# A float16 batched matmul with subtraction on one core: clearing the idle matmuls' operands on GpSimd, and another place for VectorE's first visit

## The chip, the cores and the metric

One core of one Trainium2 chip. The time is the device time of one execution in microseconds. The kernel before takes 210.94 us (median of 6 runs, 210.65 to 211.54, beside the changed kernel). The times inside a profile count from the first instruction of one profiled execution; this span (208.7 us in the kernel before) is some 2 us shorter than the device time.

## The reference

```python
batch, m, k, n = 16, 512, 1024, 768      # all float32
def reference(x, weight, sub_value):
    return (np.matmul(x, weight) - sub_value).astype(np.float32)
```

The 16 x 512 rows are 64 tiles of 128 rows. Inputs and outputs make 87 MB.

## The kernel before

SyncE issues all transfers from one queue, in a fixed order: x into a ring of 16 tiles, sub_value into a ring of 32, weights in 4 chunks, and outputs from the sub_value ring. ScalarE casts x to float16. The transposition is done by PE for most tiles and by VectorE for a pair of tiles in six. PE multiplies, and VectorE subtracts from PSUM into the ring. Three accumulators take turns.

Two parts matter here. First, PE does idle matmuls on zeros at the start, to bring its clock up before the first tile; in the kernel before, VectorE clears the zeros as the first thing of its program:

```python
starts = len(dve.ops)
dve.add(lambda: nc.vector.memset(idle_w, 0.0), then=count("idle"))
dve.add(lambda: nc.vector.memset(idle_x, 0.0), then=count("idle"))
dve.ops = dve.ops[starts:] + dve.ops[:starts]

def idle(n):
    pe.add(lambda: nc.tensor.ldweights(idle_w, tile_position=(0, 0)), [(counter["idle"], 2)])
    for _ in range(n):
        pe.add(lambda: loaded_matmul(po_b[:, NPO - 1, 0], idle_w, idle_x, start=True, stop=True))
...
idle(13)
cast(0)
pe.add(...one more idle matmul..., [(counter["ident"], 2)])
transpose_tile(0)
```

Second, PE, ScalarE and VectorE do not go straight into their work. Each first branches to the block behind it ("past"), then comes back, so that this place of its program is fetched early (called its first visit below):

```python
with nc.body("turn_head", valid_engines=engines):
    nc.br_cmp(turn, 0, on_true="past", on_false="work", comp_op="IS_EQ", engines=engines)
with nc.body("work", valid_engines=engines):
    for q in (act, dve):
        q.emit(q.ops)
    ...                                   # PE's program
    nc.br("past", engines=engines)
with nc.body("past", valid_engines=engines):
    nc.regs_alu(turn, turn, 1, op=mybir.AluOpType.add)
    nc.br_cmp(turn, 2, on_true="turn_head", on_false="rest", comp_op="IS_LT", engines=engines)
nc.switch_bb("rest")
```

## Time and profile before

| | kernel before |
|---|---|
| profiled span | 208.7 us |
| PE busy | 196.2 us, 94% |
| DMA queue of all transfers | 97.9% of 16 engines' span, 417 GB/s |
| VectorE's wait after its first branch | 3.99 us |
| idle matmuls start | 6.07 us |
| last subtraction starts | 204.08 us |
| last output issued, landed | 205.06, 207.37 us |

The first page line of the prediction below is PE's busy tenths in 40 equal slices. DMA in the second is the mean over 16 engines.

### The profile page before, as it was taken

To read this page: it belongs to the slowest core of one execution; us is meant where nothing else is said; L and a number is where in the kernel's file an instruction comes from. 1 tells how busy PE (TensorE), PEld (TensorE's weight loads), DVE (VectorE), ACT (ScalarE), POOL (GpSimd) and SP (SyncE) were. 2 spreads that over 40 slices of the span, in tenths; PEclk is the share of its full clock that TensorE was granted. 3 is DMA by queue.
4 is the path that set the end of the run, shared out by engine and by line. 5 is a ranking of instruction groups with operands and counts; after the bars stand their busy time and mean duration, and the time that the engine had idled before them with its cause. 6 is when DMAs were issued, how large, how long until landed. Compare 5 with 4: busy or idle time off the path is not lost.

```text
span 208.7 us, 2630 instructions
## 1 busy us (share of the span) xinstructions
PE 196.2 (94%) x1234; PEld 75.6 (36%) x700; DVE 127.6 (61%) x218; ACT 108.9 (52%) x113; POOL 0.8 (0%) x7
## 2 busy tenths in 40 slices
PE   0899979999999999999999999999999999999991
PEld 0023324434433443443443344344344334434430
DVE  0231151995696599299469559929946955982331
ACT  2246478554762845557276284555727629434510
POOL 1000000000000000000000000000000000000000
PEclk9999999999999999999999999999999999999997
DMA  6999999999999999999999999999999999999985
GB/s 205 407 426 429 436 422 433 443 419 437 438 422 457 400 438 443 446 427 407 460 433 415 424 429 433 441 440 432 416 452 415 435 424 429 438 438 419 423 350 211
DMA packets 5476, 87.08 MB, mean 417 GB/s; under 512 B 608, under 2 KB 608, under 8 KB 1888
## 3 DMA queue, kind: packets, MB, share of 16 engines
q1 hardware_dynamic: 5472, 87.03, 97.9%
q14 instruction: 3, 0.02, 0.1%
q8 instruction: 1, 0.02, 0.0%
HBM read 61.87 MB, written 25.17 MB: 417 GB/s over the span
## 4 chain that ended last, share of the span: by engine, by line
PE 92%; ACT 3%; issue 2%; DVE 1%; DVEq 0%; SPq 0%
PE po_b L181 82%; PE pt_b L318 10%; ACT x_b L300 1%; ACT xt_b L331 1%; ACT xtp_b L331 0%; DVE so_ring L400 0%; DVE idle_x L411 0%; DVE idle_w L410 0%; DVEq L507 0%; DVEq L519 0%; DVEq L518 0%; DVEq L555 0%; DVEq L504 0%; SPq L133 0%
## 5 line engine op out<-in xcount | busy, mean ns | idle before, releaser
L181 PE MATMUL po_b<-w_sb,xt_b 128*128 128x384 f16 x704 | 125.9, 326 | 0.0
L400 DVE TENSOR_TENSOR so_ring<-po_b,so_ring 128x768 f32<-128x768 f32 x64 | 61.2, 958 | 60.0 <-PE po_b L181 53.8
L331 ACT COPY xt_b<-pt_b 128x1024 f16<-128x1024 f16 x44 | 44.5, 1012 | 80.3 <-PE pt_b L318 79.0
L351 DVE STREAM_TRANSPOSE xtp_b<-x16p_b 32x256 f32<-32x256 f32 x144 | 62.7, 435 | 2.2
L181 PE MATMUL po_b<-w_sb,xtp_b 128*128 128x384 f16 x320 | 61.3, 326 | 0.1
L380 PEld LDWEIGHTS <-xt_b 128*128 128x128 f16 x352 | 34.4, 98 | 57.2 <-issue 53.7
L318 PE MATMUL pt_b<-ident,x_b 128*128 128x128 f32 x184 | 47.6, 274 | 1.6 <-ACT x_b L300 1.4
L300 ACT CAST x_b<-x_ring 128x1024 f16<-128x1024 f32 x46 | 47.2, 1048 | 2.9 <-DMA x_ring<-in_x_dram 2.9
L318 PEld LDWEIGHTS pt_b<-ident,x_b 128*128 128x128 f32 x184 | 25.4, 141 | 46.1 <-issue 42.4
L380 PEld LDWEIGHTS <-xtp_b 128*128 128x128 f16 x160 | 15.7, 98 | 18.5 <-issue 16.4
L300 ACT CAST x16p_b<-x_ring 128x1024 f16<-128x1024 f32 x18 | 18.8, 1046 | 4.0 <-DMA x_ring<-in_x_dram 4.0
L181 PE MATMUL po_b<-idle_x,idle_w 128*128 128x512 f16 x26 | 9.2, 513 | 6.1 <-DVE idle_x L411 6.1
L248 DVE CAST w_sb<-so_ring 128x768 f16<-128x768 f32 x8 | 4.1, 556 | 9.6 <-DMA so_ring<-in_weight_dram 9.6
L410 DVE MEMSET idle_w<- 128x64 uint32 x1 | 0.1, 112 | 5.6 <-issue 5.6
L331 ACT COPY xtp_b<-pt_b 128x1024 f16<-128x1024 f16 x2 | 2.0, 1012 | 2.2 <-PE pt_b L318 2.2
L415 PEld LDWEIGHTS <-idle_w 128*128 128x128 f16 x4 | 0.4, 99 | 6.1 <-DVE idle_x L411 6.1
L300 ACT ACT_TABLE_LOAD x1 | 1.3, 1283 | 1.8 <-issue 1.8
L487 ACT CAST stub<-ident 128x1 f16<-128x1 f32 x2 | 0.4, 196 | 0.0
L170 POOL TENSOR_SCALAR_AFFINE_SELECT ident<-ident 128x128 f32<-128x128 f32 x1 | 0.3, 292 | 0.1
L411 DVE MEMSET idle_x<- 128x256 uint32 x1 | 0.3, 272 | 0.0
L464 POOL MEMSET mark<- 128x1 f32 x1 | 0.1, 99 | 28.6 <-ACT xtp_b L331 28.6
L169 POOL MEMSET ident<- 128x128 f32 x1 | 0.2, 204 | 0.5 <-SPq L133 0.5
(4 smaller groups left out, 0.4 us busy)
## 6 DMA issues: line engine op xcount, KB each, us to landing
so_ring<-in_sub_value_dram SPq DMA_DIRECT2D x7, 3072.0 KB, 24.3
out_dram<-so_ring SPq DMA_DIRECT2D x7, 3072.0 KB, 24.5
x_ring<-in_x_dram SPq DMA_DIRECT2D x5, 4096.0 KB, 20.7
x_ring<-in_x_dram SPq DMA_DIRECT2D x2, 2048.0 KB, 27.1
so_ring<-in_weight_dram SPq DMA_DIRECT2D x4, 768.0 KB, 9.6
x_ring<-in_x_dram SPq DMA_DIRECT2D x1, 3072.0 KB, 24.8
x_ring<-in_x_dram SPq DMA_DIRECT2D x2, 1024.0 KB, 23.2
out_dram<-so_ring SPq DMA_DIRECT2D x1, 1920.0 KB, 7.7
```

What stands on the lines that cost most here:

```text
L170: pool.add(lambda: nc.gpsimd.affine_select(out=ident, in_=ident, compare_op=mybir.AluOpType.not_equal, fill=1.0, base=0, pattern=[[-1, P]] ...
L181: return nc.tensor.add_instruction(mybir.InstMatmult(name=nc.get_next_instruction_name(), engine=full.engine, ins=list(full.ins), outs=lis ...
L248: lambda at=at, r=r, st=st: nc.vector.tensor_copy(out=w_sb[:, at, r], in_=st[:, r]),
L300: act.add(lambda: nc.scalar.copy(out=to, in_=x_in), waits, count("cast"))
L318: pe.add(lambda: nc.tensor.transpose(words, from_, ident), waits, count("turn") if last else None)
L331: act.add(lambda: nc.scalar.copy(out=to, in_=pt_b[:, b]), waits, count("evac"))
L351: dve.add(lambda: nc.vector.transpose(xt[b * Q : (b + 1) * Q, :, a * Q : (a + 1) * Q], x16[a * Q : (a + 1) * Q, :, b * Q : (b + 1) * Q],), ...
L380: pe.add(lambda weights=weights: nc.tensor.ldweights(weights, tile_position=(0, 0)), [w for w in waits if w[0] in ready])
L400: dve.add(lambda: nc.vector.tensor_tensor(out=o, in0=po[:, :, :NS], in1=o, op=mybir.AluOpType.subtract), [landed["s", mi], (counter["mul"] ...
L411: dve.add(lambda: nc.vector.memset(idle_x, 0.0), then=count("idle"))
L415: pe.add(lambda: nc.tensor.ldweights(idle_w, tile_position=(0, 0)), [(counter["idle"], 2)])
L487: lambda t=t: nc.scalar.copy(out=stub[:, t - n_mt : t - n_mt + 1], in_=ident[:, :1]), [(counter["ident"], 2)], count("cast")
```

## The change

The intent: PE should not wait for VectorE's long visit. GpSimd, which is free at once, clears the operands; VectorE visits a place 140 operations into its program instead of its end.

```diff
+NEAR = 140
...
+    pool.add(lambda: nc.gpsimd.memset(idle_w, 0.0), then=count("idle"))
+    pool.add(lambda: nc.gpsimd.memset(idle_x, 0.0), then=count("idle"))
     pool.add(lambda: nc.gpsimd.memset(ident, 0.0), then=count("ident"))
...
-    starts = len(dve.ops)
-    dve.add(lambda: nc.vector.memset(idle_w, 0.0), then=count("idle"))
-    dve.add(lambda: nc.vector.memset(idle_x, 0.0), then=count("idle"))
-    dve.ops = dve.ops[starts:] + dve.ops[:starts]
...
-        for q in (act, dve):
-            q.emit(q.ops)
+        act.emit(act.ops)
+        dve.emit(dve.ops[:NEAR])
...
     nc.switch_bb("rest")
+    dve.emit(dve.ops[NEAR:])
```

## The prediction

> **What bounds the kernel now.** I read the page's busy strip first, then the chain of waits over the first 14 us, the timeline of the same stretch, the windows of the last 14 us, the DMA issues one by one, and VectorE's timeline around 35 to 48 us.
>
> From the page:
>
> ```profile
> PE   0899979999999999999999999999999999999991
> DMA  6999999999999999999999999999999999999985
> DMA packets 5476, 87.08 MB, mean 417 GB/s; under 512 B 608, under 2 KB 608, under 8 KB 1888
> ```
>
> Two things are full together. PE is busy from 30.4 us to 204.05 us without a hole, and so are the DMA engines from 2 us to 202 us (windows of 30 to 190 us give 430 to 435 GB/s at a busy share of 1.0). So an earlier start of PE isn't by itself an earlier end: the data comes no sooner.
>
> The chain of waits at the head (start, duration, what):
>
> ```profile
> 1.04 0.06 DVEq L507
> 1.11 3.99 issue
> 5.10 0.05 DVEq L518
> ...
> 5.63 0.11 DVE idle_w L410
> 5.74 0.00 issue
> 5.74 0.28 DVE idle_x L411
> 6.03 0.05 issue
> 6.07 6.09 PE po_b L181 x14
> 12.17 0.45 PE pt_b L318 x4
> ```
>
> VectorE branches to the end of its program at 1.04 us and gets its next instruction only at 5.10 us. It then comes back (0.4 us), clears the two operands, and PE starts its 14 idle matmuls at 6.07 us, ends them at 12.17 us, and only then transposes the first tile. That tile had been ready since 6.95 us:
>
> ```profile
> 5.91 1.04 ACT L300 CAST x_b<-x_ring 128x1024 f16<-128x1024 f32 x1 [2.85 <-DMA x_ring<-in_x_dram]
> 7.79 1.03 DVE L248 CAST w_sb<-so_ring 128x768 f16<-128x768 f32 x2 [1.78 <-DMA so_ring<-in_weight_dram]
> ...
> 18.73 1.03 DVE L248 CAST w_sb<-so_ring 128x768 f16<-128x768 f32 x2 [3.34 <-DMA so_ring<-in_weight_dram]
> ```
>
> So the head hangs on VectorE's late start now; the last two lines say what waits behind it: weights whose DMAs land at 7.8 us (chunk 0) and 18.7 us (chunk 3) whatever PE does.
>
> **What the Trainium skill says.** "Runtime: NRT & Kernel Launch", section Instruction fetch mechanics: most engines hold two blocks of 256 instructions, and a taken branch outside them fetches the target block by DMA before anything runs. The trace agrees: VectorE stood for 3.99 us after its branch, and the way back took only 0.24 us from branch to branch; ScalarE, with a shorter program, took 0.39 us for the same way out. "TensorE: Matmul & The Clock Gate", Part 1: the array runs at half rate until a free-running window of some 3.4 us has been busy. The trace agrees with the kind: idle matmuls start 427 ns apart up to 11.6 us and 216 ns apart from 12.4 us, a flip 5.5 to 6 us after the first one. "VectorE: DVE Perf Modes", Zero memsets can be issued as uint32: this is how VectorE clears 512 halves in 272 ns; the trace shows the 256 uint32. "DMA: Bandwidth & Descriptors", Where 436 GB/s comes from, gives a port ceiling of 435 GB/s and a lower limit near 358 for reads from HBM; the trace's 430 to 435 GB/s lies at the first, not the second. So I hold the DMA stream to be at its ceiling.
>
> **The change part by part.**
>
> 1. *GpSimd clears the operands.* Added there: two memsets ahead of the identity's. Its 128x128 memset took 204 ns and a 128x1 one 98 ns, so an element costs about (204-98)/127 = 0.83 ns, and 512 columns about 0.52 us. An estimate from these rows: start 0.94 us, idle_w done at 1.15, idle_x at 1.7, the identity (0.50 us now) at 2.2. Removed: 0.4 us of VectorE. PE is through its own branches at 1.99 us, so its idle matmuls start at about 2.0 instead of 6.07 us: 4.0 us earlier. They end near 8.0 us, after the cast (6.95 us) and after the identity.
>
> 2. *What is left of the 4.0 us after the weights.* Matmuls by weight chunk 3 need its cast, which ends at 18.73+1.03 = 19.76 us and can't come sooner. Before, they started at 22.73 us. With PE 4 us earlier everything ahead of them is done by 19.1 us (chunk 2 cast at 15.38 us, five groups of 0.65 us, one transposition of 0.45 us). So 22.73-19.76 = 3.0 us are left here.
>
> 3. *What is left after sub_value tiles 4 to 7.* Their DMA is issued at 8.22 us and lands 26.5 us later (second line below), at 34.7 us; with a full DMA stream it keeps that time. VectorE's subtraction of tile 4 waits for it now and will then:
>
> ```profile
> 34.83 0.96 DVE L400 TENSOR_TENSOR so_ring<-po_b,so_ring 128x768 f32<-128x768 f32 x1 [3.58 <-DMA so_ring<-in_sub_value_dram]
> so_ring<-in_sub_value_dram SPq DMA_DIRECT2D x1, 1536.0 KB, 26.5
> 36.58 0.96 DVE L400 TENSOR_TENSOR so_ring<-po_b,so_ring 128x768 f32<-128x768 f32 x1 [0.79 <-PE po_b L181]
> ...
> 44.80 1.79 DVE L351 STREAM_TRANSPOSE xtp_b<-x16p_b 32x256 f32<-32x256 f32 x4
> 42.56 5.36 PE L181 MATMUL po_b<-w_sb,xt_b 128*128 128x384 f16 x32
> 47.76 0.49 PE L181 MATMUL po_b<-w_sb,xtp_b 128*128 128x384 f16 x2
> ```
>
> From there VectorE works back to back: tile 5 follows tile 4 at 35.70 us instead of 36.58 (back-to-back subtractions of 26.25 us start 0.875 us apart), then 16 transposes and two subtractions. So its transposed pair, tiles 10 and 11, is done 0.87 us sooner, at 45.7 instead of 46.6 us. PE took that pair at 47.65 us, about 1.05 us after it was done. So PE can be earlier at tile 10 by 0.87+1.05, less 0.1 us for the semaphore: **1.8 us**. The 3.0 us shrink to this.
>
> 4. *After that.* I went through the later landings (issue plus time to landing): x 16 at 49.4, x 24 at 73.8, x 32 at 98.0, sub_value 8 at 47.0, 40 at 136.8, 56 at 185.3 us. Each is met by a buffer of two or three tiles (three accumulators, pairs cast seven tiles ahead); 1.8 us uses up no slack fully. The tightest is sub_value 56: the subtraction ends at 186.3 us, and tile 59, which needs its accumulator, starts at 189.65 us now, 187.8 us then. So PE ends at 202.2 instead of 204.05 us.
>
> 5. *The tail.* The windows of the end (interval, length, busy by engine, clock, DMA share, GB/s):
>
> ```profile
> 197.00:198.00 1.00, 1.00 (x9) 0.46 (x5) 0.00 (x0) 0.00 (x0) 0.00 (x0) 1.00 0.75 316
> ...
> 202.00:203.00 1.00, 1.00 (x8) 0.29 (x3) 0.43 (x1) 0.00 (x0) 0.00 (x0) 1.00 0.30 123
> 203.00:204.00 1.00, 1.00 (x7) 0.20 (x2) 0.00 (x0) 0.00 (x0) 0.00 (x0) 1.00 0.74 310
> ...
> 205.00:206.00 1.00, 0.00 (x0) 0.00 (x0) 0.04 (x1) 0.00 (x0) 0.00 (x0) 1.00 0.35 138
> ```
>
> The DMA idles for 0.25+0.70+0.26+0.65 = 1.86 us here, waiting for the last subtractions. That is all that the stream can give: everything else is 87.08 MB at its ceiling. The last outputs then run closer together: tiles 56 to 60 are sent at 194.9 us but behind older traffic, and done near 202.0; tiles 61 and 62 follow to 203.8; tile 63, issued at 203.25 us, moves from 204.1 us (now 206). So PE's 1.8 us and the DMA's 1.9 us meet, and the end comes 1.7 us sooner.
>
> 6. *The nearer place to visit.* The branch at 1.04 us goes to operation 140 of 216 rather than past the last. VectorE's trace has 243 instructions in all, so its code is about one block long and crosses one border somewhere. If the border lies ahead of operation 140 (two chances in three by length), the visit still fetches the same block and costs the same 4 us; if not, VectorE goes on in 0.3 us. Neither matters at the head: its first work waits for weights that land at 7.8 us. Cost 0; it is a risk only in mid-program (below).
>
> Sum: 211.03 - 1.7 = **209.3 us**.
>
> **The rivals.** *A, the whole 4 us arrives*: 207.0 us. For it: the chain of waits runs straight through VectorE's 3.99 us. Against it: the DMA strip, and the weight landing at 18.7 us, which alone takes 1 us off. *B, nothing arrives*: 211.0 us, if the DMA is so full that the tail stays as it is, for instance because outputs are held by uneven engines rather than by PE. For it: 97.9% busy over the span. Against it: the idle 1.86 us of the tail, each right ahead of a late issue. *C, VectorE now crosses the border unvisited in mid-run*, at operation 140 near 134 us, behind a full DMA stream: 4 us or more of standing. Pairs have about 1 us of slack and accumulators 3 to 4, so PE would lose 1 to 3 us and the time be 210.5 to 212.5 us. For it: the fetch of 3.99 us when the DMA was nearly empty. Against it: the sequential fetch ahead that the skill's page describes, and 130 us in which to do it. I give C one chance in ten.
>
> **Range and chances.** The 1.7 us can become 2.3 if landings come a little earlier, or 1.0 if one of the slacks of step 4 is less than I read; C makes the upper tail. So 208.7 to 211.0 us. Faster by over 2% means under 206.8 us, more than rival A: 0.02. Slower by over 2% means over 215.3 us, past C: 0.02. Within 2%: 0.96.
>
> **What would show it.** Step 1: idle matmuls at 2.0 us, first transposition near 8.0. Step 2: the first matmuls of weight chunk 3 right after 19.8 us. Step 3: the subtraction of tile 4 still at 34.8 us behind its DMA, tile 5 at 35.7, and PE at tile 10 with a hole ahead of it, near 45.9 us. Step 5: PE ends at 202.2 us and the windows of the tail have less idle DMA. Step 6: no hole in VectorE's timeline around 130 to 145 us. I am wrong if sub_value 4 lands earlier than 34 us, if the identity or operands come after 3 us, or if VectorE stands in mid-program.

## More of the kernel before

The chain of work that ended last, by engine and by line, is this in the kernel before (shares of the span):

```profile
PE 92%; ACT 3%; issue 2%; DVE 1%; DVEq 0%; SPq 0%
```

It names PE for nearly all of it and no DMA at all.

## The result

The changed kernel takes 210.80 us (median of 6 runs, 210.58 to 210.96); the ratio to the kernel before is 0.999, 95% interval 0.9976 to 1.0005. A ratio here is the mean time of one kernel's fast runs over that of the other's fast runs of the same rounds, so not quite the ratio of the medians. The forecast 209.3 us, with a range from 208.7 to 211.0, contains the measured time, but the gain of 1.7 us that was forecast did not come: the interval allows 0.5 us at most (0.0024 of 210.9 us).

From the page of the changed kernel, the two strips that the prediction shows for the kernel before:

```profile
PE   6998799979999999999999999999999999999960
DMA  6999999999999999999999999999999999999993
```

PE starts a slice earlier and stops about a slice earlier; the DMA strip is the same but for its last two slices.

The head of the changed kernel, from its timeline (start, duration, engine, line, operation; in brackets the idle time before and what ended it):

```profile
1.08 0.53 POOL L171 MEMSET idle_x<- 128x512 f16 x1
2.05 5.90 PE L184 MATMUL po_b<-idle_x,idle_w 128*128 128x512 f16 x14 [2.05 <-POOL idle_x L171]
7.79 0.60 PE L321 MATMUL pt_b<-ident,x_b 128*128 128x128 f32 x4
...
18.59 1.03 DVE L251 CAST w_sb<-so_ring 128x768 f16<-128x768 f32 x2 [3.35 <-DMA so_ring<-in_weight_dram]
19.67 2.11 PE L184 MATMUL po_b<-w_sb,xt_b 128*128 128x384 f16 x12 [0.54 <-DVE w_sb L251]
```

Idle matmuls start 4.0 us earlier, the first transposition 4.2 us earlier (before: 12.00 us). The weights take the first part of this lead, as forecast: matmuls of chunk 3 wait until 19.67 us (before: 22.73). Then sub_value, VectorE's pair and tile 10, from the timelines of VectorE and of PE:

```profile
34.66 1.82 DVE L403 TENSOR_TENSOR so_ring<-po_b,so_ring 128x768 f32<-128x768 f32 x2 [5.88 <-DMA so_ring<-in_sub_value_dram]
43.76 1.79 DVE L354 STREAM_TRANSPOSE xtp_b<-x16p_b 32x256 f32<-32x256 f32 x4
45.79 0.81 PE L184 MATMUL po_b<-w_sb,xtp_b 128*128 128x384 f16 x4 [1.09 <-DVE xtp_b L354]
```

The DMA of sub_value 4 to 7, in the view of DMA issues, is this:

```profile
so_ring<-in_sub_value_dram SPq DMA_DIRECT2D x1, 1536.0 KB, 25.8
```

Issued at 8.72 us, it lands at 34.57 us (before: 34.74). The subtraction of tile 4 stays where that puts it, and PE meets the hole of 1.09 us ahead of tile 10. After it the view shows no hole of PE to the end. The last subtraction shows what reaches the tail, the kernel before first, then the changed one:

```profile
204.08 0.96 DVE L400 TENSOR_TENSOR so_ring<-po_b,so_ring 128x768 f32<-128x768 f32 x1 [1.64 <-PE po_b L181]
```

```profile
202.11 0.96 DVE L403 TENSOR_TENSOR so_ring<-po_b,so_ring 128x768 f32<-128x768 f32 x1 [1.64 <-PE po_b L184]
```

So 1.97 us of PE's lead arrive at the last subtraction, and none of it at the end of the program. What lies between is one output transfer. The DMA issues of the last output, before and after (KB, us from issue to landing):

```profile
out_dram<-so_ring SPq DMA_DIRECT2D x1, 384.0 KB, 2.3
```

```profile
out_dram<-so_ring SPq DMA_DIRECT2D x1, 384.0 KB, 4.7
```

Issued at 203.10 instead of 205.06 us, it takes 4.7 instead of 2.3 us. The chain of the changed kernel, by engine, now names DMA for 12%, the early sub_value load; the slow landing at the end it does not name:

```profile
PE 75%; DMA 12%; DVE 6%; SPq 3%; issue 1%; DVEq 0%
```

And the windows of the tail (interval, length, busy of PE, weight load, VectorE, ScalarE, GpSimd with counts, PE clock, DMA share, GB/s); first a row of the kernel before that the prediction does not show, then the changed kernel:

```profile
206.00:207.00 1.00, 0.00 (x0) 0.00 (x0) 0.00 (x0) 0.00 (x0) 0.00 (x0) 0.77 0.89 353
```

```profile
202.00:203.00 1.00, 0.07 (x1) 0.00 (x0) 0.89 (x1) 0.00 (x0) 0.00 (x0) 1.00 0.94 393
203.00:204.00 1.00, 0.00 (x0) 0.00 (x0) 0.07 (x1) 0.00 (x0) 0.00 (x0) 1.00 1.01 421
204.00:205.00 1.00, 0.00 (x0) 0.00 (x0) 0.00 (x0) 0.00 (x0) 0.00 (x0) 1.00 0.91 369
205.00:206.00 1.00, 0.00 (x0) 0.00 (x0) 0.00 (x0) 0.00 (x0) 0.00 (x0) 0.77 0.33 135
206.00:207.00 1.00, 0.00 (x0) 0.00 (x0) 0.00 (x0) 0.00 (x0) 0.00 (x0) 0.50 0.15 61
```

The idle gaps of 202 to 204 us are closed, as forecast: the stream is nearly full to 205 us. But then it does not stop. A share of 0.33 and then 0.15 of 16 engines goes on for 2 us, as if some five, then two or three engines were still at it. The records of single packets bear this out: in the changed kernel four packets are in flight around 205.9 us, three around 206.4, and one alone from 206.8 to 207.2. In the kernel before, exactly three are in flight at 202.9 to 203.2 us and again at 205.4 to 205.7, while the rest have nothing to move, and there is none at all for only 0.05 us, at 205.84.

That can be looked at engine by engine. The Trainium skill, "DMA: Bandwidth & Descriptors", section Why a DMA increments its semaphore by 16 and not by 1, says that each of up to 16 DMA engines adds one when its own share has landed. The trace agrees: each of the 38 transfers has 16 separate increments. The times of the first, the eighth and the last of them, taken from the trace:

```
                        kernel before                 changed kernel
transfer             first   eighth    last       first   eighth    last
x 0                   4.09     4.35    5.88        3.95     4.41    5.99
sub_value 56-63     183.19   183.54  185.31      183.24   183.65  185.27
out 48-55           197.73   198.06  199.87      197.76   198.19  200.31
out 56-60           202.53   202.63  204.39      202.29   202.74  204.93
out 61-62           205.53   205.62  206.25      204.12   204.57  206.77
out 63              207.19   207.28  207.37      205.23   205.49  207.75
```

In the first transfer the last of the 16 is already 1.8 to 2.0 us behind the first, and in these two kernels this is never made up: from 8 to 195 us 16 packets or more are in flight for all but 0.3 to 0.5 us, so no engine pauses in which it could catch up. (Neither increments nor packets carry an engine's number; that every engine gets the same bytes, and that it is the same engine that comes last, is inferred from the nearly constant distance.) In the changed kernel three engines end 1.8 to 2.5 us late, and the rest within 1.2 us. Follow the last column of the changed kernel: 4.62, 1.84 and 0.98 us from one output to the next, for 123, 49 and 25 KB per engine if the bytes are shared evenly, which is 25 to 27 GB/s. A packet of 24.6 KB took 0.912 us in the middle of the run, 27 GB/s. So this engine has no gap that these numbers show. In the kernel before, the same column has 4.52, 1.86 and 1.12 us: here too its gap is only 1.12 - 0.98 = 0.14 us. Its first column has 3.00 us from outputs 56-60 to 61-62, where 49 KB take 1.8 us, and 1.66 us from there to the last, where 25 KB take 0.9. So the idle time of the tail was nearly all that of the quick engines.

**Theory:** the slowest of the 16 DMA engines is busy from 2 us to the end in both kernels, but for some 0.1 us, so PE's lead only turns the wait for PE into a wait for that engine. **Rivals:** (a) the nearer visit, with a fetch in mid-run, costs what the clearing wins; (b) a fixed cost in the tail holds the end; (c) the lag between engines is only how they start, and has nothing to do with instruction fetches.

### The profile page after: what moved, and what is told of

It is laid out like the page before. It is cut to its first block, busy times and chain, and to the rows that moved or that the text cites. A ratio compares the mean times of both kernels' runs of the same rounds, so it can differ in the third digit from the quotient of the medians.

```text
span 209.0 us, 2630 instructions
## 1 busy us (share of the span) xinstructions
PE 196.5 (94%) x1234; PEld 75.5 (36%) x700; DVE 127.0 (61%) x216; ACT 109.0 (52%) x113; POOL 1.4 (1%) x9
## 4 chain that ended last, share of the span: by engine, by line
PE 75%; DMA 12%; DVE 6%; SPq 3%; issue 1%; DVEq 0%
PE po_b L184 67%; DMA so_ring<-in_sub_value_dram 12%; PE pt_b L321 8%; DVE xtp_b L354 3%; DVE so_ring L403 2%; SPq L284 2%; SPq L248 1%; SPq L554 0%; DVEq L60 0%; SPq L134 0%
## 5 line engine op out<-in xcount | busy, mean ns | idle before, releaser
L383 PEld LDWEIGHTS <-xtp_b 128*128 128x128 f16 x160 | 15.7, 98 | 19.8 <-issue 17.7
L171 POOL MEMSET idle_x<- 128x512 f16 x1 | 0.5, 530 | 0.0
L462 POOL MEMSET mark<- 128x1 f32 x1 | 0.1, 99 | 24.6 <-ACT xtp_b L334 24.6
```

What stands on the lines that cost most here:

```text
L171: pool.add(lambda: nc.gpsimd.memset(idle_x, 0.0), then=count("idle"))
L383: pe.add(lambda weights=weights: nc.tensor.ldweights(weights, tile_position=(0, 0)), [w for w in waits if w[0] in ready])
```

## The experiments

### Each half of the change alone

`pool_only`, the visit at the end again:

```diff
-NEAR = 140
+NEAR = 10**6
```

> Only the clearing by GpSimd; VectorE visits the end of its program first, as in the kernel before. Theory (the slowest of the 16 DMA engines is never idle and sets the end): VectorE gets on at 5.1 us again, its weights land at 7.8 us, so PE's lead stays 1.97 us, PE ends near 202.1 us, and the time is 210.8 us, within 0.4 us of both kernels. Rival (the nearer visit, with its fetch at 162 us in mid-run, ate the gain): without it the time falls to 209.0 us or less.

Measured: 210.80 us, ratio 1.0000 (0.9984 to 1.0017), correct. VectorE gets on at 5.16 us, its weights still come at 7.90 us, idle matmuls start at 2.05 us, and the last subtraction at 202.31 us. Rival (a) falls: without the nearer visit nothing comes back. All of this is as expected.

`near_only`, the clearing on VectorE again (two more operations, so 142), as seen from the changed kernel:

```diff
-NEAR = 140
+NEAR = 142
-    pool.add(lambda: nc.gpsimd.memset(idle_w, 0.0), then=count("idle"))
-    pool.add(lambda: nc.gpsimd.memset(idle_x, 0.0), then=count("idle"))
+    ...the four lines of the kernel before, on nc.vector...
```

> Only the nearer place to visit; VectorE clears the operands, as in the kernel before. Theory: VectorE is back from its visit at about 2.0 us, clears both operands by 2.5 us, so PE starts idle matmuls near 2.5 us instead of 6.07: the visit alone gives PE nearly all of the lead, PE ends near 202.1 us, and the time stays within 0.4 us of 210.8. Rival (GpSimd's clearing is what moves PE): PE still starts at 6 us.

Measured: 210.98 us, ratio 1.0005 (0.9989 to 1.002), correct. From its timeline:

```profile
2.14 0.11 DVE L411 MEMSET idle_w<- 128x64 uint32 x1 [2.14 <-issue]
```

The visit alone moves the clearing from 5.63 to 2.14 us and PE's start to 2.58 us; the last subtraction starts at 202.17 us. Either half gives the lead, the two together no more than one, and neither gives time.

### DMA to spare

`before_light` and `after_light` load only half of the last four sub_value transfers, 6.3 MB less. Results are wrong (relative error 0.50).

```diff
+            if kind == "s" and at >= NSO:
+                here, there = here[:, : n // 2], there[:, : n // 2]
             if kind == "o":
                 here, there = there, here
```

> The kernel before with half of the last four sub_value loads left out (6.3 MB of 87.1, results wrong on purpose), so the DMA has about 14 us to spare. Theory: the kernel before is held by PE and by the DMA at once, PE a hair later, so it ends at 210.7 us, at most 0.4 us sooner than before; PE ends at 204.0 us.

> The changed kernel with the same 6.3 MB left out (results wrong on purpose). Theory: with DMA to spare PE's lead of 1.97 us reaches the end: last output issued at 203.1 us and landed 2.3 us later, time 208.8 us, ratio to the kernel before 0.990. Rival (a fixed cost of the tail or of the nearer visit holds the end): no difference to the light form of the kernel before, 210.6 us.

Measured: `after_light` 208.62 us, ratio 0.990 (0.9883 to 0.9916), as the theory had it. The last subtraction of its profiled run starts at 202.05 us, as in the changed kernel (202.11), and the last output takes 2.3 us again (its line reads as that of the kernel before, above).

So with nothing changed on PE's side, less DMA alone lets PE's lead through. Rival (b) falls with it: no fixed cost of the tail holds the end. The increments show the lag from its other side. In `after_light` one packet alone is in flight from 179.5 to 182.1 us, and the last increment of outputs 40 to 47 comes 3.42 us after the first. Then no packet is in flight for 0.3 us. After that pause the 16 increments of each of the last four outputs come within 0.12 to 0.17 us. In `before_light`, after a pause of 2.7 us from 180.4 us, it is 0.17 to 0.18. So the lag goes once all engines have run dry.

`before_light` was a miss: 209.80 us, ratio 0.9956 (0.9941 to 0.9971), where at most 0.4 us of gain were expected; and its runs spread from 209.18 to 210.35 us. The reason shows in its head:

```profile
6.07 4.81 PE L181 MATMUL po_b<-idle_x,idle_w 128*128 128x512 f16 x14 [6.07 <-DVE idle_x L413]
```

The same 14 idle matmuls from the same start took 4.81 us here and 6.09 us in the profiled run of before: they start 427 ns apart at first and 216 ns apart later, and the change came at 9.4 us here and only after 11.6 us there. PE was 1.3 us ahead, and its last subtraction started at 202.79 us. Over the eleven profiled runs the 14 matmuls took from 4.47 to 6.09 us. So in the kernel before, too, PE is early in some runs, and with all bytes to move the end makes no use of it: it was held by both, and the profiled run happened to be one with a late change.

The lead of the changed kernel with DMA to spare is then 0.9956 - 0.990 = 0.0056 of 210.9 us, 1.2 us, not 2.0. This fits the heads: in the changed kernel PE waits for weights and for VectorE's pair ahead of tile 10 whenever the change comes (14 idle matmuls took 4.99 us in `after_light` and 5.90 in the changed kernel, the last subtraction started within 0.06 us), while in the kernel before an early change is worth up to 1.3 us. No run tested this change, or PE's clock, by itself.

### A little DMA at a time

`after_less1` and `after_less2` leave out one and two tiles of the last sub_value load, `before_less2` two. Results are wrong.

```diff
+            if kind == "s" and at == 56:
+                here, there = here[:, : n - 1], there[:, : n - 1]      # n - 2 in the others
```

> The changed kernel with one tile fewer in the last sub_value load (0.39 MB of 87.1; results wrong on purpose). At 0.43 MB per us that is 0.91 us of DMA. Theory (the changed kernel is held by its slowest DMA engine alone): the whole 0.9 us comes off, 210.8 to 209.9 us. Rival (a fixed cost of the tail, which many megabytes less only happened to lift): no change, 210.8 us.

> The same with two tiles fewer, 0.79 MB or 1.83 us of DMA. Theory: 210.8 - 1.8 = 209.0 us; from there on PE, which ends at 202.1 us, is the bound (the light form gave 208.6), so this is nearly all that there is.

> The kernel before with the same two tiles fewer. Theory: it is held by the DMA only a little, so 1.8 us of DMA less give 1.1 us as in its light form, 209.8 us; the changed kernel is then ahead of it by 0.8 us or more, where with all bytes it is ahead by 0.1.

Measured:

```
                MB less   ratio (95%)               median   last output, issue to landing
changed            0      0.9990 (0.9976-1.0005)    210.80   4.7
after_less1        0.39   0.9978 (0.9966-0.9991)    210.37   4.0
after_less2        0.79   0.9926 (0.9912-0.9940)    209.28   3.0
after_light        6.3    0.9900 (0.9883-0.9916)    208.62   2.3
before_less2       0.79   0.9970 (0.9955-0.9985)    210.23   2.8
before_light       6.3    0.9956 (0.9941-0.9971)    209.80   2.3
```

The direction and the order are the theory's: each tile less brings the last landing nearer to its 2.3 us while the last subtraction stays at 202.0 us. The sizes are partly off. One tile less was to give 0.9 us; its profiled span is 0.7 us shorter (208.3 against 209.0), but the timed runs give 0.4 us by medians, and its interval overlaps with that of the changed kernel, which was timed in other rounds: this step alone is not clear of noise. Two tiles less give 1.5 us by medians of the 1.8 expected, clear of it. `before_less2` came to 210.23 us, where 209.8 was expected: a miss by 0.4 us. The lags of single engines differ from run to run (the last of the 16 increments of outputs 61 and 62 came 2.65 us after the first in the changed kernel, 2.32 in `pool_only`, 2.78 in `near_only`), so the dose is not a clean one. Against the kernel before at the same dose, the changed one is ahead by 0.9970 - 0.9926 = 0.0044, 0.9 us, where 0.8 or more was expected. These runs take bytes from all engines alike. They show that the DMA holds the end; that its late engines are what holds it rests on the increments and the packets in flight. No run took the lag away and left the bytes.

### Where the lag comes from

`no_visit` is the changed kernel without first visits:

```diff
-    nc.regs_mov(turn, 0)
+    nc.regs_mov(turn, 1)
```

> The changed kernel without any first visit: the branch register starts at 1, so the three engines run straight into their work. It asks whether the instruction fetches at 2.0 to 4.9 us are what puts single DMA engines behind. Theory: without them the spread of a transfer's 16 landings falls from 1.9 us to about 1 us at the first weights, but the fetches come later, in mid-run and behind a full stream, and some engine stands for it: time 210 to 213 us. Rival (the spread comes from the engines' different start, not from fetches): the spread stays at 1.9 us.

Measured: 210.78 us, ratio 1.0002 (0.9985 to 1.0019), correct. Packets of instruction fetches in the two traces, and the last minus the first of a transfer's 16 increments:

```
changed kernel: fetch packets at 2.00 (8 KB, 1.65 us), 3.97 (8 KB, 0.31 us), 3.97 (16 KB, 0.93 us), 162.15 (8 KB, 0.32 us)
no_visit:       fetch packets at 31.09 (16 KB, 1.07 us), 57.11, 79.46, 160.95 (8 KB each, 0.31 to 0.34 us)

last minus first, us     x 0   weights 1   x 8-11   sub_value 4-7   x 56-63   out 63
changed kernel           2.04     1.89      1.86         1.86         2.18      2.51
no_visit                 0.92     0.95      0.96         1.86         2.08      2.55
```

Rival (c) falls for the first part of the lag: without the early fetches the spread starts at 0.92 us and stays there, until the 16 KB fetch at 31.09 us, and the very next transfer has 1.86 us. In it one increment alone came late: the other 15 lay within 0.94 us. The jump of 0.90 us is nearly the length of that fetch. The 0.92 us that are there without any fetch stay unexplained. The Trainium skill, "DMA: Bandwidth & Descriptors", section Queues, rings and completion order, says that each DMA engine takes turns among its rings and that one ring row of the runtime does refills; the trace agrees for the 8 KB fetches, which are packets of queue 14, and in that one engine of the data queue falls behind at a fetch; the 16 KB fetch is of queue 8, though. But PE, ScalarE or VectorE was expected to stand for a late fetch, and none did: the view puts none of their waits over 0.15 us down to "issue" (no cause that the profile shows), and the time is the same. The spread at the end is about the same too, 2.55 us. Between 145 and 190 us one or two further engines fall back by 0.6 to 1.0 us in the traces of the kernel before, the changed kernel and `no_visit`; the one fetch packet of 0.3 us that the last two hold there does not explain it, and the kernel before has none there. That part of the lag stays open.

`probe` sends the last output tile of the changed kernel in six pieces, each of which uses another set of DMA engines (a piece of 2 partitions uses two, and so on):

```diff
+PIECES = ((0, 2), (2, 6), (6, 14), (14, 29), (29, 125), (125, 128))
...
+            if kind == "o" and at == n_mt - 1:
+                for i, (lo, hi) in enumerate(PIECES[:-1]):
+                    ...one dma_start of out_dram[lo:hi] for each, with its own semaphore...
```

> The changed kernel with the last output tile sent in six pieces of 2, 4, 8, 15, 96 and 3 partitions, so that each piece uses another subset of the 16 DMA engines. If the laggards are always the same low-numbered engines, the first pieces land 2 us late already; if they are high-numbered, the pieces of 2 to 8 partitions land at once (2.2 us after their issue) and the one of 96 is late. The time should stay within 1 us of 210.8.

Measured: 211.55 us (one look, state unknown, correct). Times of the increments; the first of each is the one that stands for engines not used:

```
partitions   issued   landings
2            202.88   203.32 | 204.67 205.07
4            203.25   203.68 | 204.68 204.85 205.25 206.67
8            203.56   204.07 | 205.02 to 205.42 (six) 206.60 206.86
15           203.94   204.44 | 205.31 to 205.68 (twelve) 206.53 206.80 207.05
96           204.31            206.35 to 206.75 (thirteen) 207.19 207.34 207.53
3            204.74   205.22 | 206.59 206.69 206.78
```

Neither of the two expectations holds: there are none late of 2 or of 3, one of 4, two of 8, three of 15 and three of 16. So three engines are late, spread over the set, the same three for all pieces if each larger set holds the smaller ones (inferred, as before). Only a piece of 2 or 3 partitions leaves out all of them, so this gave no way to a faster kernel. No version with right results beat both kernels.

## Why the prediction was wrong

- *Step 1, GpSimd's clearing*, was right: idle_x cleared at 1.61 us (forecast 1.7), idle matmuls at 2.05 us (2.0), first transposition at 7.79 us (8.0).
- *Step 2, what the weights leave*, was right: 19.67 us (19.8).
- *Step 3, what sub_value 4 leaves*, was right: subtraction at 34.66 us (34.8), the hole ahead of tile 10, and tile 10 at 45.79 us (45.9). One reading was off: PE took that pair at 47.76 us before, as the line that the prediction shows says, and not at 47.65, so the lead is 1.97 and not 1.8 us.
- *Step 4, PE ends at 202.2 us*, was right: the last subtraction starts at 202.11 us.
- *Step 6, the visit*, was right in its cost: the visit took 0.50 us (1.11 to 1.61, where the kernel before has 3.99), so it was the case given one chance in three. There is no hole at operation 140: VectorE's transposes at 127.68 and 128.13 us follow at their usual pace. Rival C did not come.
- *Step 5, the tail*, is the step that failed: "The DMA idles for 0.25+0.70+0.26+0.65 = 1.86 us here ... That is all that the stream can give". The sum is a mean over 16 engines. The slowest had 0.14 us to give. "Tile 63, issued at 203.25 us, moves from 204.1 us" held for the quick engines, whose landings came from 205.23 us on, and not for the slow three, which landed at 207.02 to 207.75. This is rival B, which the prediction named with its right cause ("outputs are held by uneven engines rather than by PE") and then set aside by the very figure that hides it, a mean share. That the measured time lies inside the stated range was no success of the mechanism: the gain did not come.
- The view that would have shown it was there in the trace of before: the 16 increments of each transfer, 1.79 us apart in the first one and 1.87 us in outputs 56 to 60.
- *Rival A* was rightly put aside; its weight argument is step 2.
- The size: the kernel before has 0.14 us of gap in its slowest engine; the changed kernel's slowest engine ended 0.38 us later (207.75 against 207.37) as its lag was larger (2.65 against 2.14 us at most, in the last outputs), while timed runs gained 0.1 us. That difference between one profiled run and the timed ones is inside the spread of lags from run to run.

## What to carry to other kernels

When the DMA is full and a mean busy share shows a little idle time at the end, ask what the slowest engine does: compare the increments of one transfer's semaphore, first to last. Where a lag as large as that idle time never shrinks, as here, the slowest engine has no idle time to give, and a lead won elsewhere ends there. Before forecasting a gain from a chain that names only PE, take a small part of the DMA away: if the time falls, PE is not alone.

## What the Trainium skill lacked or had wrong

- "Runtime: NRT & Kernel Launch", Instruction fetch mechanics, calls the cost of crossing a block mostly hidden. For the engine that executes the runs agree (no hole in VectorE's work around the fetch at 162.15 us; its gaps there are 0.03 us at most). What the page leaves out is the DMA engine that carries the fetch: in `no_visit` a 16 KB fetch of 1.07 us came just before one engine's increments fell 0.90 us behind, and 120 us of full stream later the spread was still 1.76 us.
- The same section gives blocks of 16 KiB; the traces hold 8 KB packets also by themselves (8.30 us in the kernel before, 162.15 us in the changed one). Whether such a packet is a whole block, no run shows.
- "DMA: Bandwidth & Descriptors", Where 436 GB/s comes from, says without a condition that between HBM and SBUF a limit near 358 GB/s binds; only another section of the page ties that figure to both cores of a pair streaming. Here, with one core at work, 87 MB went at 417 GB/s over the whole span and at 430 to 435 in the middle.
- "DMA: Bandwidth & Descriptors", Latency and other measured facts, names engines 7 and 15 as the slower ones, for descriptors that GpSimd makes. Here, with SyncE's, three engines lag by 1.8 to 2.5 us in the last output; the piece for 15 engines has all three of them and leaves out one that is not late.
- No page says how the lag of single DMA engines is read from a transfer's 16 increments, nor that a mean share hides it: 0.30 in the kernel before at 202 to 203 us, while its slowest engine had 0.14 us of gap in the whole tail.
